# A two-block transformer kernel in float32r: SBUF buffers of matmul operands moved to multiples of 512 bytes

## Chip, cores and metric

The program runs on one core of a Trainium2 chip, in one launch. The metric is device time in microseconds, the median of several executions. In the texts TensorE is PE in the profile's rows, its weight loads PEld, VectorE DVE, ScalarE ACT, GpSimd POOL, and the queue of SyncE SP.

## The reference

One sequence of 512 tokens with 1024 features goes through two blocks of dense products and attention, in float32. Cut to what matters:

```python
def first_block(x, mem, ...):          # two layers
    for i in range(2):
        # layer 0: short convolution with gates, layer 1: window attention with sinks
        y_mem = _mem_attention(q_mem, mk, mv)
        x = x + jnp.concatenate([y_tok, y_mem], -1) @ w_out
        h = rmsnorm(x, norm_ffn[i])
        x = x + (jax.nn.silu(h @ w_gate[i]) * (h @ w_up[i])) @ w_down[i]   # 1024 -> 2816 -> 1024
    return rmsnorm(x, final_norm)

def second_block(x, ...):
    proj = rms_norm(x, norm_pre) @ w_in     # then compressed/causal attention and retention
    merged = sigmoid(m_a) * (y_n @ w_nsa_o) + sigmoid(m_b) * (y_r @ w_ret_o)
    return x + rms_norm(merged @ w_out, norm_post)
```

## The kernel before

Activations lie feature-major: a tile of 128 partitions (features) by 512 columns (tokens), eight such tiles for 1024 features. Every dense product is done to nearly float32's precision with three passes in float32r. Both operands are split into a high part that float32r holds exactly and a low part (the rest), and `mm3` (lines 108 to 113) adds high*high (line 111), high weight*low activation (line 112) and low weight*high activation (line 113) in PSUM. Each of the three is one matmul: its stationary operand, a block of 128x128 weights, is loaded into the array first (a weight load, a row on PEld), and its moving operand, 512 columns of activations, streams through it. So a weight load goes with every matmul, even in line 112, which loads the block that line 111 had loaded.

`proj` (lines 115 to 122) makes a product of 128 output features by 512 tokens: one call of `weights` for a [128, 1024] slab of weights, then three matmuls for each of its eight chunks k, 24 in all (21 or 24 where the hidden layer of a feed-forward part is taken in groups of 8, 7 and 7 chunks). `proj_tok` (lines 124 to 136) is the other way round: it makes 128 tokens by 256 (or 280) features, so that the activations are stationary and 256 columns of weights stream.

`weights` (lines 94 to 106) sets how far ahead the work runs: a DMA on SP brings the slab into one of two buffers `wr`, ScalarE copies it rounded to float32r into one of three buffers `wh` (line 65), VectorE writes the rest into one of three buffers `wl` (line 75). The buffers of a tag go round in turn, so three products in a row use all three pairs of `wh` and `wl`. The order of the work is that of the program as the Tile framework puts it down, with semaphores between engines.

Where the buffers lie: pools are laid out one behind the other in each partition: constants (`cst`, starting at byte 16512), the weight buffers (`wp`), the activation slots (`sl`, mostly of 512 floats, that is 2048 bytes each), and small columns (`sm`). A weight buffer has WMAX = 1120 floats = 4480 bytes, which is 8.75 times 512. The addresses in the built program, with what is left over by 512:

| buffer | address in a partition | modulo 512 |
|---|---|---|
| wh, first, second, third | 34464, 38944, 43424 | 160, 32, 416 |
| wl, first, second, third | 47904, 52384, 56864 | 288, 160, 32 |
| every 2048-byte slot of `sl` (activations, h, q, k, x) | 61344 and on, each a whole number of 2048 | 416 |
| the four `v` slots (values) | 202656 and on | 416 |
| zero, ones; ident | 17792, 17280; 16512 | 384, 384; 128 |

Chunk k of a slab lies 512 k bytes further, so all chunks of a buffer have the same remainder. Products that the steps of the prediction name, by the buffer pair in the built program: the one that starts at 823.58 us uses the third pair, that at 829.13 the second, that at 834.74 the first, that at 840.28 the third again.

Of the kernel before, what the change touches and what calls it, by code (L numbers as in the profile page):

```python
# [8 lines left out]
F32 = mybir.dt.float32  # L9
# [9 lines left out]
D = 1024  # L19
NC8 = 8  # L20
NMEM = 256
NEG = -1.0e30
WMAX = 1120
KWORDS = 2 * 9 * 64
# [3 lines left out]
class Build:  # L28
    """Feature-major activations [128 features, 512 tokens]; every dense product is three float32r
    passes over an exact high/low split of both operands (hi*hi + hi*lo + lo*hi)."""  # L30

# [13 lines left out]

# [1 line left out]
    def nm(self, s):  # L47
# [14 lines left out]

# [1 line left out]
    def copy(self, out, in_, scale=1.0):  # L64
# [14 lines left out]
    def split_one(self, x, tag, scale=None, n=256, name="s"):  # L79
        """Both parts in one tile."""  # L80
        t = self.slot(tag, F32R, (128, KWORDS) if tag == "v" else (128, 512), name)
        hi, lo = t[:, :n], t[:, n:2 * n]
        self.copy(hi, x, 1.0 if scale is None else scale)
        self.lo_of(lo, x, hi, scale)
        return hi, lo
# [8 lines left out]
    def weights(self, src, nk, nn, parts=1):  # L94
        """One load of [128, nk*nn] weights and its split."""
        nc, n = self.nc, nk * nn
        raw = self.wp.tile([128, WMAX], F32, name=self.nm("wr"), tag="wr", bufs=self.wbufs["wr"])
        hi = self.wp.tile([128, WMAX], F32R, name=self.nm("wh"), tag="wh", bufs=self.wbufs["wh"])
        lo = self.wp.tile([128, WMAX], F32R, name=self.nm("wl"), tag="wl", bufs=self.wbufs["wl"])
        step = n // parts  # L100
        for s in (slice(a, a + step) for a in range(0, n, step)):
            nc.sync.dma_start(raw[:, s], src[:, s] if parts > 1 else src)
        for s in (slice(a, a + step) for a in range(0, n, step)):
            self.copy(hi[:, s], raw[:, s])
            self.lo_of(lo[:, s], raw[:, s], hi[:, s])
        v = lambda t: t[:, :n].rearrange("p (k c) -> p k c", k=nk)
        return v(hi), v(lo)
# [7 lines left out]
    def proj(self, ps, src, rhs, w=None, order=None):  # L115
        """ps[128 columns, tokens] = W^T h over all chunks of rhs (8 at most)."""
        n = ps.shape[1]
        wh, wl = w or self.weights(src, len(rhs), 128)
        order = order or range(len(rhs))
        for k in order:  # L120
            ah, al = rhs[k]
            self.mm3(ps, wh[:, k], wl[:, k], ah[:, :n], al[:, :n], k == order[0], k == order[-1])

    def proj_tok(self, src, rhs, nn, ntb, done, nk=4, tag=("pp",)):
        """done(tb, ps[128 tokens, nn]) for each block of 128 tokens."""
        units = [self.weights(src[:, j], nk, nn) for j in range(len(rhs) // nk)]
# [10 lines left out]

# [1 line left out]
    def square_sum(self, chunks, n=512, first=False, gain2=None, tags=("sa", "s")):  # L139
        """The chunks' squares summed by column; with gain2 (squared gains) also their weighted sum."""  # L140
        nc = self.nc
# [18 lines left out]
    def token_mean(self, acc, n, eps, div):  # L160
        """[128 tokens, n/128] of the column sums of acc over div, plus eps."""
        nt = n // 128
# [7 lines left out]
    def rsqrt(self, v):  # L170
        """Newton's iteration from the exponent's halving."""
        nc, n = self.nc, v.shape[1]
# [10 lines left out]
    def newton(self, z, t, y, v):  # L183
        """z = y (1.5 - v y^2 / 2)."""
        self.stt(t, y, -0.5, y, ALU.mult, ALU.mult)
        self.mul(t, t, v)
        self.stt(z, t, 1.5, y, ALU.add, ALU.mult)

    def spread(self, rs, name):
        """[128 tokens, nt] to a row of tokens on every partition."""  # L190
        nc, nt = self.nc, rs.shape[1]
# [12 lines left out]

# [1 line left out]
    def stack_q(self, x):  # L206
        """The two heads of x [128, n], each as its high part on its own half and its low part on the other."""
        n = x.shape[1]
# [8 lines left out]
    def stack_k(self, x, packed=False, tag="b"):  # L217
        """For each head of x [128, n]: its high part on both halves, and its low part on both."""
        n = x.shape[1]
# [22 lines left out]
    def fill_values(self, v, ps, rs):  # L242
        """ps [128 tokens, 4*64] scaled by rs, split, between columns of zeros."""
        hi, lo = v[:, 0, 1::2], v[:, 1, 1::2]
        src = ps.rearrange("p (h c) -> p h c", c=64)
        self.copy(hi, src, rs)
        self.lo_of(lo, src, hi, rs)

    def transposes(self, parts, n):
        """parts: (column, source [128, 128]); the transposed blocks, split."""  # L250
        ps = self.psum("tp")
# [16 lines left out]
    def last_value(self, ps, rs):  # L268
        """The last block of values as they are, for the products too narrow for float32r."""
        v = self.slot("v3", F32, (128, 576), "v3").rearrange("p (j c) -> p j c", c=64)  # L270
# [10 lines left out]
    def scaled(self, p, r):  # L281
        """p *= r, by row."""
        self.nc.vector.tensor_scalar(p, p, r, None, op0=ALU.mult)

# [1 line left out]
    def load_consts(self):  # L286
        nc, T = self.nc, self.T
        self.ident = self.const("ident", [128, 128])
        self.gains = self.const("gains", [128, 8 * 8])
        self.ones = self.const("ones", [128, 128])  # L290
        nc.vector.memset(self.ones, 1.0)
# [26 lines left out]
    def bias_tables(self, loaded):  # L318
        """[128 queries, 12 heads, 256 keys] of the band's bias, -1e30 outside of the window."""
        nc, T = self.nc, self.T  # L320
# [18 lines left out]
    def mem_rows(self, tag="pb"):  # L339
        """The memory times its norm's gain, split; its scale by token at the first call."""  # L340
        nc, T = self.nc, self.T
# [40 lines left out]
    def mem_attention(self, qs, ks, vs):  # L382
        """qs: the two pairs' stacked queries; returns the split outputs of the pairs."""
        nc = self.nc
# [29 lines left out]
    def queries(self, src, h, R, rope=None):  # L414
        """A pair of heads' queries, over 8 and stacked."""
        ps = self.psum("pp")
# [164 lines left out]

# [1 line left out]
    def rope(self, x, tables, shuffle):  # L583
        """x * cos + partner(x) * sin."""
        nc = self.nc
# [17 lines left out]
    def silu(self, ps, R, tag):  # L603
        """z sigmoid(z) as (1 + tanh(z/2)) z/2."""
        z = self.halfsilu_pre(ps, R)
# [5 lines left out]
    def compress(self, kT, j):  # L611
        """The blocks' first product: [2 groups * 31 blocks, 256 hidden]."""
        nc, T = self.nc, self.T
# [25 lines left out]
    def compress_gelu(self, ps, j):  # L639
        """gelu of it, transposed: [128, 2, 2 groups, 32]."""  # L640
        nc = self.nc
# [55 lines left out]
    def cmp_probs(self, g, qpair):  # L697
        """The gated probabilities of group g over the compressed keys, transposed: [4 heads * 32, 512]."""
        nc = self.nc
# [218 lines left out]
    def gate_tanh(self, i, h, R, tag):  # L918
        """tanh of half a merge gate's preactivation: block i // 2 of m_a or m_b."""
        ps = self.psum("pp")  # L920
# [6 lines left out]
    def gate_ahead(self, h, R):  # L927
        """The next merge gate, to DRAM: it keeps TensorE busy beside the softmax."""
        i = len(self.mt)
# [11 lines left out]
    def outer_x(self, c):  # L941
        """Block c of x * gf * rs1, by token, to DRAM."""
        nc = self.nc
# [10 lines left out]
    def finish(self, merged):  # L954
        """out = x * gf * rs1 + rmsnorm(merged @ w_out) by token."""
        nc, T = self.nc, self.T
# [19 lines left out]
        for tb in range(4):  # L976
            v, sd, y0, t, ri = (self.small(1, name=n) for n in ("fv", "fd", "fy", "ft", "fr"))
            nc.vector.tensor_reduce(v, ss[tb], op=ALU.add, axis=AX.X)
# [27 lines left out]

# [1 line left out]
def _feat(w):  # L1008
    """[K, C] to [C/128, 128, K]: per block of columns, each partition's rows of all chunks."""
    k, c = w.shape  # L1010
# [3 lines left out]
def _tok(w, nk=4):  # L1014
    """[K, C] to [128, K/(128 nk), nk*C]."""
    k, c = w.shape
# [3 lines left out]
def _chunks(x):  # L1020
    """[tokens, D] to [128, D/128, tokens]."""
    t, d = x.shape
    return np.ascontiguousarray(x.T.reshape(d // 128, 128, t).transpose(1, 0, 2))
# [36 lines left out]
def _pack(i):  # L1060
    """The arrays that the program reads, laid out."""
    w = {n: np.asarray(a) for n, a in i.items()}
# [62 lines left out]
```

## Time and profile before

| | |
|---|---|
| median of three executions | 1693.08 us (1692.97 to 1693.48) |
| span of the profiled execution | 1692.4 us, 21,221 instructions; of its own time nothing but the span is recorded |
| TensorE busy | 1661.1 us (98%), 8184 matmuls |
| granted TensorE clock, mean | 0.994 |
| weight loads busy | 1378.0 us (81%) |
| VectorE, ScalarE, GpSimd busy | 1055.8, 639.2, 250.5 us |

Matmuls are pipelined. A row's duration runs from its start to a modelled end that lies in the next matmul, so for TensorE's pace one reads the distance from one start to the next; a longer duration shows there too. The weight load of the next matmul runs beside the matmul before it.

### The profile page before, as it was taken

How to read it: one execution, taken by the hardware profiler on the slowest of the kernel's cores; microseconds unless marked ns; L12 is line 12 of the kernel's file. 1: busy time of each engine (PE TensorE's matmuls, PEld its weight loads, DVE VectorE, ACT ScalarE, POOL GpSimd, SP SyncE). 2: the span in 40 equal slices, each digit the busy share in tenths (PEclk: the TensorE clock that was granted, in tenths of full speed). 3: DMA queues.
4: the chain of work that ended last, by engine and by line, in shares of the span. 5: the costliest groups of instructions: out<-in, count | busy, mean ns of one | idle time of the engine just before them, and what ended most of it. 6: DMA issues, size and time to landing. Idle time of an engine off the chain costs nothing.

```text
span 1692.4 us, 21221 instructions
## 1 busy us (share of the span) xinstructions
PE 1661.1 (98%) x8184; PEld 1378.0 (81%) x8184; DVE 1055.8 (62%) x1828; ACT 639.2 (38%) x1134; POOL 250.5 (15%) x220
## 2 busy tenths in 40 slices
PE   8999999999999999999999999999999999999997
PEld 6887878888888788887888888887788888888887
DVE  7765754444454979875434434589788977764444
ACT  5532332222232467633222222334466533333233
POOL 1111411002011600041000101251001000010010
PEclk9999999999999999999999999999999999999999
DMA  5322222322352422122322322332411122143342
GB/s 186 118 83 98 89 89 99 100 88 92 108 168 86 154 90 78 67 100 87 100 89 98 105 95 94 97 135 87 167 41 57 45 81 82 69 149 112 124 157 88
DMA packets 51557, 171.39 MB, mean 101 GB/s; under 512 B 6680, under 2 KB 6880, under 8 KB 51328
## 3 DMA queue, kind: packets, MB, share of 16 engines
q1 hardware_dynamic: 45504, 151.11, 26.4%
q0 software_dynamic: 5376, 18.82, 3.4%
q8 instruction: 64, 1.05, 0.3%
q14 instruction: 37, 0.30, 0.1%
q10 hardware_dynamic: 576, 0.11, 0.0%
HBM read 160.56 MB, written 11.81 MB: 102 GB/s over the span
## 4 chain that ended last, share of the span: by engine, by line
PE 83%; DVE 9%; issue 3%; ACT 2%; DMA 1%; POOL 1%; SPq 0%; DVEq 0%; ACTq 0%; POOLq 0%
PE pp L112 11%; PE pp L113 11%; PE pp L111 11%; PE lg L112 8%; PE lg L113 8%; PE lg L111 7%; PE tp L112 3%; PE tp L113 3%; PE tp L111 3%; PE po L111 2%; PE tp L253 2%; PE po L112 2%; PE po L113 2%; DVE wl L75 2%; PE pp L133 1%
## 5 line engine op out<-in xcount | busy, mean ns | idle before, releaser
L65 ACT ACTIVATE wh<-wr 128x1024 fp32r<-128x1024 f32 (+2 forms) x280 | 288.2, 1029 | 717.9 <-PE pp L112 226.5
L75 DVE TENSOR_TENSOR wl<-wr,wh 128x1024 fp32r<-128x1024 f32 (+2 forms) x280 | 384.6, 1374 | 52.6 <-ACT wh L65 49.4
L111 PE MATMUL pp<-gh,wh 128*128 128x512 f32 x880 | 349.0, 397 | 7.8 <-ACT wh L65 7.2
L113 PE MATMUL pp<-gh,wl 128*128 128x512 f32 x880 | 353.2, 401 | 0.6 <-DVE wl L75 0.6
L112 PE MATMUL pp<-gl,wh 128*128 128x512 f32 x880 | 351.8, 400 | 0.4 <-DVE gl L71 0.4
L111 PEld LDWEIGHTS pp<-gh,wh 128*128 128x128 f32 x880 | 168.9, 192 | 45.7 <-ACT wh L65 8.1
L112 PEld LDWEIGHTS pp<-gl,wh 128*128 128x128 f32 x880 | 166.5, 189 | 37.0 <-DVE gl L71 1.1
L113 PEld LDWEIGHTS pp<-gh,wl 128*128 128x128 f32 x880 | 166.6, 189 | 35.1 <-DVE wl L75 1.6
L113 PE MATMUL lg<-gh,wl 128*128 128x512 f32 x408 | 162.0, 397 | 0.0
L112 PE MATMUL lg<-gl,wh 128*128 128x512 f32 x408 | 161.9, 397 | 0.0
L111 PE MATMUL lg<-gh,wh 128*128 128x512 f32 x408 | 160.6, 394 | 0.0
L68 POOL TENSOR_TENSOR u<-u,z 128x512 f32<-128x512 f32 x44 | 64.6, 1469 | 563.6 <-DVE u L68 375.9
L68 DVE TENSOR_TENSOR u<-lg,Rf 128x512 f32<-128x512 f32 x44 | 30.4, 691 | 144.2 <-PE lg L113 144.1
L111 PEld LDWEIGHTS lg<-gh,wh 128*128 128x128 f32 x408 | 77.7, 190 | 18.5 <-issue 0.5
L112 PEld LDWEIGHTS lg<-gl,wh 128*128 128x128 f32 x408 | 76.6, 188 | 18.9 <-issue 0.7
L113 PEld LDWEIGHTS lg<-gh,wl 128*128 128x128 f32 x408 | 76.6, 188 | 17.1 <-issue 0.2
L112 PE MATMUL tp<-actl,wh 128*128 128x512 f32 x216 | 85.9, 398 | 0.5
L113 PE MATMUL tp<-acth,wl 128*128 128x512 f32 x216 | 85.8, 397 | 0.0
L111 PE MATMUL tp<-acth,wh 128*128 128x512 f32 x216 | 84.4, 391 | 0.0
L68 DVE TENSOR_TENSOR z<-pp,Rf 128x512 f32<-128x512 f32 x44 | 30.4, 691 | 74.6 <-PE pp L113 70.8
L503 DVE TENSOR_TENSOR x<-x,tp 128x512 f32<-128x512 f32 x36 | 24.6, 684 | 68.3 <-PE tp L113 68.3
L71 DVE SCALAR_TENSOR_TENSOR gl<-x,gains,gh 128x512 fp32r<-128x512 f32 x40 | 52.9, 1337 | 0.5 <-ACT gh L65 0.5
(422 smaller groups left out, 3096.6 us busy)
## 6 DMA issues: line engine op xcount, KB each, us to landing
wr<-in_w_gate_dram SPq DMA_DIRECT2D x44, 512.0 KB, 3.2
wr<-in_w_up_dram SPq DMA_DIRECT2D x44, 512.0 KB, 3.2
wr<-in_w_in_dram SPq DMA_DIRECT2D x44, 512.0 KB, 3.3
wr<-in_w_down_dram SPq DMA_DIRECT2D x32, 448.0 KB, 3.3
wr<-in_a_w_in_dram SPq DMA_DIRECT2D x18, 512.0 KB, 3.2
wr<-in_w_down_dram SPq DMA_DIRECT2D x16, 512.0 KB, 3.5
wr<-in_a_w_out_dram SPq DMA_DIRECT2D x8, 512.0 KB, 3.2
wr<-in_b_w_q_dram SPq DMA_DIRECT2D x8, 512.0 KB, 3.2
```

The costliest lines, as they stand in the source:

```text
L65: self.nc.scalar.activation(out, in_, AF.Copy, scale=scale)
L68: (eng or self.nc.vector).tensor_tensor(out, a, b, op=ALU.mult)
L71: (eng or self.nc.vector).scalar_tensor_tensor(out, a, s, b, op0=op0, op1=op1)
L75: self.nc.vector.tensor_tensor(out, x, hi.bitcast(F32), op=ALU.subtract)
L111: mm(ps, ah, bh, start=start, stop=False)
L112: mm(ps, ah, bl, start=False, stop=False)
L113: mm(ps, al, bh, start=False, stop=stop)
L133: mm(ps, a, wh, start=k == 0, stop=False)
L253: self.nc.tensor.transpose(ps[:, c:c + 128], src, self.ident)
L503: nc.vector.tensor_tensor(self.x[c], self.x[c], ps, op=ALU.add)
```

## The change

It puts a constant tile `pad` of 88 floats (352 bytes) behind `gains`, which shifts what follows it; gives the `wh` and `wl` buffers 1152 floats (4608 bytes, 9 times 512) in place of 1120, while `wr`, which no matmul reads, keeps 1120; and takes the five small columns per token block at the end of the program (`fv`, `fd`, `fy`, `ft`, `fr`) from buffers that other steps used earlier, which frees the space. Comments and docstrings are emptied as well.

```diff
-WMAX = 1120
+WMAX = 1152
...
-        raw = self.wp.tile([128, WMAX], F32, name=self.nm("wr"), tag="wr", bufs=self.wbufs["wr"])
+        raw = self.wp.tile([128, 1120], F32, name=self.nm("wr"), tag="wr", bufs=self.wbufs["wr"])
         hi = self.wp.tile([128, WMAX], F32R, name=self.nm("wh"), tag="wh", bufs=self.wbufs["wh"])
         lo = self.wp.tile([128, WMAX], F32R, name=self.nm("wl"), tag="wl", bufs=self.wbufs["wl"])
...
         self.gains = self.const("gains", [128, 8 * 8])
+        self.const("pad", [128, 88])
         self.ones = self.const("ones", [128, 128])
...
-            v, sd, y0, t, ri = (self.small(1, name=n) for n in ("fv", "fd", "fy", "ft", "fr"))
+            v, sd, y0, t, ri = (self.small(4, name=n)[:, :1] for n in ("nm", "den", "es", "rec", "m"))
```

In the built program every engine has the same instructions in the same order, with the same semaphores and waits; only addresses and the row width of `wh`, `wl` and the five columns differ. Now `wh` lies at 34816, 39424 and 44032, `wl` at 48640, 53248 and 57856, and the slots from 62464 on: all of them multiples of 512. Not so the constants: ones and zero have a remainder of 224, ident stays at 128; the small copies `k3` have 256.

## Rows read from the trace of the kernel before

**Rows 1.** The page's span and busy time of each engine.

```profile
span 1692.4 us, 21221 instructions
PE 1661.1 (98%) x8184; PEld 1378.0 (81%) x8184; DVE 1055.8 (62%) x1828; ACT 639.2 (38%) x1134; POOL 250.5 (15%) x220
```

**Rows 2.** The page's chain that ended last, share of the span by engine.

```profile
PE 83%; DVE 9%; issue 3%; ACT 2%; DMA 1%; POOL 1%; SPq 0%; DVEq 0%; ACTq 0%; POOLq 0%
```

**Rows 3.** Engines by stretch: time, then each engine's busy time (count), clock, DMA.

```profile
200.00:560.00 360.00, 359.57 (x1595) 292.79 (x1594) 174.09 (x202) 109.44 (x143) 41.97 (x36) 1.00 0.32 104
...
1560.00:1692.40 132.40, 123.19 (x727) 108.38 (x725) 56.15 (x95) 41.67 (x77) 13.42 (x19) 0.98 0.36 122
```

**Rows 4.** TensorE in time order: start us, us, line; first matmuls of four products.

```profile
823.58 0.39 PE L111 MATMUL pp<-gh,wh 128*128 128x512 f32 x1
...
829.13 0.40 PE L111 MATMUL lg<-gh,wh 128*128 128x512 f32 x1
...
834.74 0.39 PE L111 MATMUL pp<-gh,wh 128*128 128x512 f32 x1
...
840.28 0.39 PE L111 MATMUL lg<-gh,wh 128*128 128x512 f32 x1
```

**Rows 5.** Engines by stretch, 12 to 16 and 800 to 850 (clock after the counts).

```profile
12.00:16.00 4.00, 3.81 (x9) 3.04 (x10) 4.00 (x8) 4.00 (x8) 0.00 (x0) 1.00 0.94 334
800.00:850.00 50.00, 50.00 (x217) 40.69 (x216) 25.75 (x23) 14.81 (x18) 6.45 (x5) 1.00 0.28 90
```

**Rows 6.** TensorE in time order among its first matmuls.

```profile
12.78 0.63 PE L113 MATMUL pp<-gh,wl 128*128 128x512 f32 x1
13.20 0.63 PE L111 MATMUL pp<-gh,wh 128*128 128x512 f32 x1
...
14.91 0.63 PE L112 MATMUL pp<-gl,wh 128*128 128x512 f32 x1
15.34 0.63 PE L113 MATMUL pp<-gh,wl 128*128 128x512 f32 x1
```

**Rows 7.** Lines 111 to 113 in 823.57 to 829.12: duration ns min/median/max.

```profile
L111 PE MATMUL pp<-gh,wh x8: 389/389/390, 823.6 to 828.4; 128*128 128x512 f32 x8
L112 PE MATMUL pp<-gl,wh x8: 396/396/397, 823.8 to 828.7; 128*128 128x512 f32 x8
L113 PE MATMUL pp<-gh,wl x8: 397/397/404, 824.0 to 828.9; 128*128 128x512 f32 x8
```

**Rows 8.** Lines 111 to 113 in 834.73 to 840.28.

```profile
L111 PE MATMUL pp<-gh,wh x8: 389/389/390, 834.7 to 839.6; 128*128 128x512 f32 x8
L112 PE MATMUL pp<-gl,wh x8: 396/396/397, 835.0 to 839.8; 128*128 128x512 f32 x8
L113 PE MATMUL pp<-gh,wl x8: 397/397/397, 835.2 to 840.1; 128*128 128x512 f32 x8
```

**Rows 9.** Lines 111 to 113 in 829.12 to 834.73.

```profile
L111 PE MATMUL lg<-gh,wh x8: 393/393/401, 829.1 to 834.0; 128*128 128x512 f32 x8
L112 PE MATMUL lg<-gl,wh x8: 395/395/398, 829.4 to 834.3; 128*128 128x512 f32 x8
L113 PE MATMUL lg<-gh,wl x8: 393/397/398, 829.6 to 834.5; 128*128 128x512 f32 x8
```

**Rows 10.** TensorE in time order, products of 256 columns: first and last of nineteen.

```profile
599.99 0.28 PE L135 MATMUL pp<-wl,gh 128*128 128x256 f32 x1
...
602.11 0.28 PE L135 MATMUL lg<-wl,gh 128*128 128x256 f32 x1
```

**Rows 11.** The page's costliest groups: the weights' split on ScalarE and VectorE.

```profile
L65 ACT ACTIVATE wh<-wr 128x1024 fp32r<-128x1024 f32 (+2 forms) x280 | 288.2, 1029 | 717.9 <-PE pp L112 226.5
L75 DVE TENSOR_TENSOR wl<-wr,wh 128x1024 fp32r<-128x1024 f32 (+2 forms) x280 | 384.6, 1374 | 52.6 <-ACT wh L65 49.4
```

**Rows 12.** Line 541 (the tile of zeros times itself): duration ns min/median/max.

```profile
L541 PE MATMUL po<-zero x6: 388/392/455, 647.2 to 709.5; 128*128 128x512 f32 x6
```

**Rows 13.** Line 111 alone by product: time, busy (count), loads, clock, DMA share, GB/s.

```profile
823.57:829.12 5.55, 3.11 (x8) 1.54 (x8) 1.00 0.18 38
829.12:834.73 5.61, 3.15 (x8) 1.50 (x8) 1.00 0.45 149
834.73:840.28 5.55, 3.11 (x8) 1.53 (x8) 1.00 0.18 43
840.28:845.84 5.55, 3.11 (x8) 1.54 (x8) 1.00 0.45 149
```

## The prediction

> **What bounds the kernel now.** I read the page first: TensorE is busy for 1661.1 us of a span of 1692.4 [rows 1], and the chain that ended last lies on TensorE for 83%, on VectorE for 9% [rows 2]. The table by stretches says where it is free of everything else: in 200 to 560 us, the first feed-forward part, it is busy for 359.57 us of 360.0; in the last 132 us, where it waits for other engines, for 123.2 [rows 3]. So time is won or lost only by the pace at which matmul follows matmul, and the change can touch nothing else: no instruction, order or wait differs, only addresses.
>
> The pace is in the rows in time order. Three products of 24 matmuls each start at 823.58, 829.13 and 834.74, and the next at 840.28 [rows 4]: 5.55, 5.61 and 5.54 us, 16.70 us for 72 matmuls, or 231.9 ns each, at a granted clock of 1.00 in that part [rows 5]. 512 columns at 2.4 GHz take 213.3 ns. So each matmul pays some 18.6 ns beyond its columns. At the start of the program that is not so: from 12.78 to 15.34 there are six steps of 427 ns [rows 6], just 512 columns at 1.2 GHz, the lower of the two levels (the clock column, with 1.00 in that stretch [rows 5], does not show it). Whatever costs the 18.6 ns is hidden at half the pace.
>
> Now the reader is to see that the extra depends on addresses. The three products are alike but for the buffer pair. In the first, with the third pair, line 111 lasts 389 ns while lines 112 and 113 last 396 and 397 [rows 7]; with the first pair it is the same [rows 8]; with the second pair line 111 lasts 393, up to 401 [rows 9], and the whole product is 0.06 us longer. The activations lie at a remainder of 416 by 512 always, that is 160 by 256. By 256 the remainders of the pairs are: first wh 160 and wl 32, second wh 32 and wl 160, third wh 160 and wl 32. A matmul's length covers the loading of the next block, so the pair to look at is its own block and the next one. Line 111 has wh, then wh again: 160 and 160 in the first and third pairs (fast), 32 and 32 in the second (slow). Line 112 has wh, then wl, line 113 wl, then wh: always one at 160 and one at 32, always slow. So of the nine kinds of step (three lines, three pairs) two are fast: those in which both blocks lie where the activations lie, by 256.
>
> Two sizes follow. With f for a fast step and s for a slow one, the second product is 24 s = 5.61, so s = 233.8 ns; the first is 8 f + 16 s = 5.55, so f = 226 ns. The difference, 7 to 8 ns, agrees with the durations, 389 against 396 or 397 [rows 7]; I take 7, with 6 and 8 as its ends since the rows are rounded to 10 ns.
>
> **The change part by part.** The wider `wh` and `wl` buffers and the `pad` act together: all weight buffers and all slots get the same remainder, 0. Then every matmul has both of its blocks where its activations lie, and by the pattern above every step is a fast one. The program has 5,762 float32r matmuls of 512 columns. Of 72 steps of three products 16 + 24 + 16 = 56 are slow, 78%, which is 4,480 matmuls; at 7 ns each, 31 us on TensorE. Not all of it reaches the end: where TensorE waits for softmax or norms, work done earlier only waits longer. I pass on the chain's share of TensorE, 83%: **26 us**. Ends: 6 ns and 83% give 22, 8 ns and all of it 36.
>
> The 1,676 float32r matmuls of 256 columns: from 599.99 to 602.11 lie 18 steps [rows 10], 118 ns each, against 106.7 for 256 columns. They mix both sorts of addresses already and I see no sorting by them in the rows; price zero, ends zero and 11 ns each, 18.6 us, times 83%: 15 us less.
>
> `wr` moves from remainders 416 and 288 to 256 and 128, so DMAs and the splits in `weights` see other addresses. ScalarE sits idle for 717.9 us before its copies (1029 ns each), and VectorE's subtractions of 1374 ns each run up to three slabs ahead of TensorE [rows 11]; a few ns on 280 of each, 1 or 2 us, would lie under TensorE. If that cover were gone in the feed-forward parts it would be those 2 us. Zero. The five columns in old buffers: they carry no added wait, and a 4-byte column at another address is at most some ns on 20 short instructions of the tail. Zero. ones, zero, ident and `k3` stay off the grid; they serve few matmuls. Zero.
>
> Sum: 1692.4 - 26 = 1666.4 on the profiled execution, which stands 0.7 us under the median of the runs (1693.08): **1667 us** forecast. With the ends of this case alone 1657 to 1672.
>
> **What could lie below.** The fast step, 226 ns, still has 13 ns beyond its columns, and today no activation starts at a multiple of 64 bytes. If the extra is made of steps of some 7 ns and one of them comes from that, all 5,762 lose 7 more: 40 us, times 83%, 33: 1634. The floor is the pace without any extra: 18.6 ns on 5,762, 107 us, times 83%, 89, and 15 from the 256 columns: 1589. The row nearest to the question speaks for staying at 226: line 541 streams the tile of zeros (remainder 384 by 512, a multiple of 128) past itself, and its six matmuls have a median of 392 and a least of 388 ns [rows 12], no shorter than the fast 389. But it streams one block of 128 columns four times, with split weights of either sort behind it, so it is no clean test. The Trainium skill (TensorE: Matmul & The Clock Gate, section Back-to-back issue gap) gives columns over 2.4 plus 2.5 ns between warm matmuls, measured 215.7 for 512 columns. By that figure, as an estimate, 16.2 ns on 5,762 times 83% would go, and the time would be 1615; no row here is that short.
>
> **Rivals.**
>
> Below the fast step: aligned streams and loads shed at least one more step of 7 ns. For it: full pace at the lower clock [rows 6], so the extra is a matter of delivery, which the start of an operand can affect. Against it: [rows 12]. Time 1634, at the extreme 1589; I put 1610 to 1640 on most of it. Chance 0.27.
>
> No change: addresses are not what sets the pace. Then what I read as buffer pairs is something else that alternates with them, the DMA beside TensorE for one: in the product with the second pair the DMA engines were busy for 0.45 of the time, in its neighbours for 0.18 [rows 13]. For it: 0.06 us of 5.55 is a small signal. Against it: the product that starts at 840.28 has a share of 0.45 as well, but the third pair, and there the eight steps of line 111 are back at 3.11 us against 3.15 [rows 13]. Time 1693, within 3. Chance 0.14. The Trainium skill backs this rival (SBUF — State Buffer, section Who interferes with whom): TensorE's two read ports, for the stream and for the loads, are independent, and it never waits on anyone. By that rule the sum would be zero; the rows disagree with it, since line 111 lengthens with the buffer from which blocks are loaded [rows 7, 9].
>
> Slower: remainder 0 is a bad place. That 160 is fast and 32 slow may be a property of the place itself and not of its agreement with the activations: the second pair's line 111 has both blocks at the same place too, and is slow [rows 9]. Loads and streams now all begin at the same phase, and if what delivers them takes turns by address, each pair meets at its first words. It decides if a step with both blocks at 0 takes 234 ns or more. Then the 22% that are fast, 1,280 matmuls, lose 7 ns: 9 us, times 83%, 7: **1700**. If all went to the longest duration of the regular steps, 401 against 396 [rows 9], 5 ns on 5,762 come on top, 24 us with the share: 1724. For it: only one fast place is known. Against it: 160 and 416 are both fast [rows 7, 8], so agreement by 256 explains the rows with one cause. Chance 0.14.
>
> **How the numbers follow.** All steps fast 0.43, below that 0.27, no change 0.14, slower 0.14, the small rest left over. The time is that of the first case, 1667. The range goes down to where 11 of the 13 ns that the fast step has left go too (11 on 5,762, 83%: 53 us under the forecast, 1614) and leaves out what lies lower, about 0.07; at the top it takes in the slow case's first price and leaves out its second, about 0.06: 1614 to 1702, with 1657 to 1672 for the likeliest case alone. A measurement of this kernel can tell about 0.2% from no change, 3.4 us: faster 0.71, same 0.14, slower 0.15.
>
> **What would show it.** Lines 111, 112 and 113 with one and the same duration near 389 ns, for all three buffer pairs; products of 24 matmuls at 5.43 us each, evenly; a stretch of 50 us of feed-forward with 221 matmuls in place of 217 [rows 5]; TensorE's busy time down by some 30 us; the split's means unchanged. The second case shows in durations of 382 and products of 5.28 us or less. I am wrong if the durations still differ between lines with all buffers alike, or if all are at 396 and more.

## The result and the profile after

The changed kernel takes 1670.18 us in the median of four executions (1668.66 to 1670.72), the kernel before 1693.03 us beside it. The ratio is 0.9865, with a 95% interval of 0.9851 to 0.9879: 1.35% faster. The forecast was 1667.

The page of the changed kernel, its span, the engines' busy time and the chain that ended last:

```profile
span 1668.7 us, 21221 instructions
...
PE 1634.9 (98%) x8184; PEld 1374.2 (82%) x8184; DVE 1059.2 (63%) x1828; ACT 639.0 (38%) x1134; POOL 247.1 (15%) x220
...
PE 82%; DVE 10%; issue 2%; ACT 2%; DMA 1%; POOL 1%; DVEq 0%; SPq 0%; ACTq 0%; POOLq 0%
```

Against [rows 1] TensorE is busy for 26.2 us less, and the span is 23.7 us shorter; the kernel has the same bound as before [rows 2]. The same four products as in [rows 4], the first matmul of each, in time order (start us, us, line):

```profile
810.17 0.39 PE L111 MATMUL pp<-gh,wh 128*128 128x512 f32 x1
...
815.61 0.39 PE L111 MATMUL lg<-gh,wh 128*128 128x512 f32 x1
...
821.05 0.39 PE L111 MATMUL pp<-gh,wh 128*128 128x512 f32 x1
...
826.49 0.39 PE L111 MATMUL lg<-gh,wh 128*128 128x512 f32 x1
```

Each product of 24 matmuls takes 5.44 us, whichever buffer pair it uses: 226.7 ns a step, against 231.9 before. Lines 111 to 113 in the first of these products, third pair of buffers (duration ns min/median/max), and in the second, second pair:

```profile
L111 PE MATMUL pp<-gh,wh x8: 389/389/389, 810.2 to 814.9; 128*128 128x512 f32 x8
L112 PE MATMUL pp<-gl,wh x8: 389/389/389, 810.4 to 815.2; 128*128 128x512 f32 x8
L113 PE MATMUL pp<-gh,wl x8: 389/389/389, 810.6 to 815.4; 128*128 128x512 f32 x8
...
L111 PE MATMUL lg<-gh,wh x8: 389/389/389, 815.6 to 820.4; 128*128 128x512 f32 x8
L112 PE MATMUL lg<-gl,wh x8: 389/389/389, 815.8 to 820.6; 128*128 128x512 f32 x8
L113 PE MATMUL lg<-gh,wl x8: 389/389/389, 816.1 to 820.8; 128*128 128x512 f32 x8
```

Where before 389 stood beside 393, 396 and 397 [rows 7, 9], every step now has the one duration that only line 111 with the first and third pairs had. It is the same over the whole program: 140 products of 24 steps run through without a wait. Before, the 92 of them on the first and third pairs took 5.54 to 5.56 us and the 48 on the second pair 5.59 to 5.61; now 134 of the 140 take 5.44. In 800 to 850 us, in the table by stretches (time, busy time and count of each engine, clock, DMA), 222 matmuls stand in place of 217 [rows 5], at the same granted clock of 1.00:

```profile
800.00:850.00 50.00, 50.00 (x222) 41.44 (x221) 24.87 (x24) 14.03 (x17) 5.17 (x4) 1.00 0.31 95
```

The split's groups keep their means, but for 1% on VectorE [rows 11]:

```profile
L65 ACT ACTIVATE wh<-wr 128x1024 fp32r<-128x1024 f32 (+2 forms) x280 | 288.5, 1030 | 695.1 <-PE pp L112 228.0
L75 DVE TENSOR_TENSOR wl<-wr,wh 128x1024 fp32r<-128x1024 f32 (+2 forms) x280 | 388.7, 1389 | 55.5 <-ACT wh L65 52.3
```

One thing got worse. The 18 steps of 256 columns that took 2.12 us [rows 10] take 2.16 now, 120 ns each:

```profile
588.77 0.28 PE L135 MATMUL pp<-wl,gh 128*128 128x256 f32 x1
...
590.93 0.28 PE L135 MATMUL lg<-wl,gh 128*128 128x256 f32 x1
```

### The profile page after: what moved, and what is told of

It is laid out like the page before. It is cut to its first block, busy times and chain, and to the rows that moved or that the text cites. A ratio compares the mean times of both kernels' runs of the same rounds, so it can differ in the third digit from the quotient of the medians.

```text
span 1668.7 us, 21221 instructions
## 1 busy us (share of the span) xinstructions
PE 1634.9 (98%) x8184; PEld 1374.2 (82%) x8184; DVE 1059.2 (63%) x1828; ACT 639.0 (38%) x1134; POOL 247.1 (15%) x220
## 4 chain that ended last, share of the span: by engine, by line
PE 82%; DVE 10%; issue 2%; ACT 2%; DMA 1%; POOL 1%; DVEq 0%; SPq 0%; ACTq 0%; POOLq 0%
PE pp L112 11%; PE pp L113 11%; PE pp L111 11%; PE lg L111 8%; PE lg L112 8%; PE lg L113 7%; PE tp L112 3%; PE tp L253 2%; PE tp L113 2%; PE tp L111 2%; DVE wl L75 2%; PE po L111 2%; PE po L112 2%; PE po L113 2%; PE pp L133 2%
## 5 line engine op out<-in xcount | busy, mean ns | idle before, releaser
L75 DVE TENSOR_TENSOR wl<-wr,wh 128x1024 fp32r<-128x1024 f32 (+2 forms) x280 | 388.7, 1389 | 55.5 <-ACT wh L65 52.3
L113 PE MATMUL pp<-gh,wl 128*128 128x512 f32 x880 | 347.2, 395 | 0.6 <-DVE wl L75 0.6
L112 PE MATMUL pp<-gl,wh 128*128 128x512 f32 x880 | 346.7, 394 | 0.5 <-DVE gl L71 0.5
L504 DVE TENSOR_TENSOR x<-x,tp 128x512 f32<-128x512 f32 x36 | 24.6, 683 | 65.5 <-PE tp L113 65.5
```

The source lines that it names most:

```text
L75: self.nc.vector.tensor_tensor(out, x, hi.bitcast(F32), op=ALU.subtract)
L112: mm(ps, ah, bl, start=False, stop=False)
L113: mm(ps, al, bh, start=False, stop=stop)
L504: nc.vector.tensor_tensor(self.x[c], self.x[c], ps, op=ALU.add)
```

## The experiments

All of them are edits of the changed kernel. "Distance" below is the address of the stationary block less that of the stream, by 256 bytes: 0, 256 and 512 bytes apart are one distance, and so are -64 and 192.

**The two halves of the change.** First the wider buffers without the pad, then the pad without the wider buffers.

```diff
# e1_wide_only
-        self.const("pad", [128, 88])
# e2_pad_only
-WMAX = 1152
+WMAX = 1120
```

> The change without its pad: wh and wl are 1152 floats wide, so weight buffers and slots all have the remainder 160 by 512, not a multiple of 512 nor of 64. Theory A (a step is fast when its own block and the next one lie where the stream lies, by 256): every step fast, about 227 ns, time as with the whole change, 1670 us. Theory M (the multiple of 512 is what counts): the slow steps stay, 1693 us.

> The change without the wider buffers: 1120 floats and the pad. wh lies at 0, 384, 256 by 512, wl at 128, 0, 384, slots at 256. Relations by 256 are those of before (wh agrees, differs by 128, agrees; wl the opposite). Theory A: 1693 us, line 111 fast in two of three products. Theory P (the place of the weight blocks alone counts, 0 and 160 by 256 being good ones): not sure to repeat before's pattern, since 128 by 256 has not been seen; theory M: between, the slots being off the grid.

e1_wide_only: 1670.52 us (1669.00 to 1671.99), ratio to before 0.9867, 0.9850 to 0.9883. Weights and slots all lie at 160 by 512, and the products follow each other as in the whole change, 5.44 us apart:

```profile
811.13 0.39 PE L111 MATMUL pp<-gh,wh 128*128 128x512 f32 x1
...
816.57 0.39 PE L111 MATMUL lg<-gh,wh 128*128 128x512 f32 x1
```

e2_pad_only: 1691.97 us in one execution, before's time. Line 111 in two products, then line 112 in the first (duration ns min/median/max):

```profile
L111 PE MATMUL pp<-gh,wh x8: 389/389/389, 823.5 to 828.3; 128*128 128x512 f32 x8
L111 PE MATMUL lg<-gh,wh x8: 393/393/401, 829.0 to 834.0; 128*128 128x512 f32 x8
...
L112 PE MATMUL pp<-gl,wh x8: 396/396/396, 823.7 to 828.6; 128*128 128x512 f32 x8
```

The medians are those of before to the nanosecond, with every address moved. So the wider buffers carry the gain, the pad carries none, and a multiple of 512 is not what counts: theory M falls.

**Is it the place or the agreement?** e3_slots_128 leaves all weight blocks on multiples of 512 and moves the activation slots alone (with the small columns behind them, which no dense product reads); e4_all_32 puts everything at 32 by 256, where the slow blocks of before had lain.

```diff
# e3_slots_128, in weights, behind lo
+        if "gap2" not in self.wbufs:
+            self.wbufs["gap2"] = self.wp.tile([128, 32], F32, name="gap2", tag="gap2", bufs=1)
# e4_all_32
-        self.const("pad", [128, 88])
+        self.const("pad", [128, 32])
```

> The whole change, and 128 bytes of padding behind the weight buffers, so that all weight blocks stay at multiples of 512 and all activation slots lie 128 bytes off. Theory A: no step agrees with its stream, all are slow, 233 to 235 ns; 5,762 steps at 7 ns, 83% of it: 33 us above the change, 1703 us. Theory P (the weight blocks' place alone): all fast, 1670 us.

> The wider buffers and a pad of 32 floats: weight buffers and slots all at 288 by 512, that is 32 by 256, where before's slow blocks lay. Theory A: all agree, all fast, 1670 us. Theory P: 32 by 256 is a bad place for a weight block, all steps 233 ns or more, 1700 us.

e3_slots_128 took 1695.56 us, e4_all_32 1669.59, one execution each, where the change took 1670.18. The page of e3_slots_128 and the starts of its four products (two lines are added ahead of `mm3`, so line 113 is what line 111 was):

```profile
span 1693.8 us, 21221 instructions
...
PE 1663.2 (98%) x8184; PEld 1375.1 (81%) x8184; DVE 1056.3 (62%) x1828; ACT 640.6 (38%) x1134; POOL 251.1 (15%) x220
```

```profile
825.35 0.39 PE L113 MATMUL pp<-gh,wh 128*128 128x512 f32 x1
...
842.08 0.39 PE L113 MATMUL lg<-gh,wh 128*128 128x512 f32 x1
```

72 steps in 16.73 us, 232.4 ns each, with no weight block moved; TensorE is busy for 28.3 us more than in the change. And in e4_all_32, in the place that had been slow, the same products are 5.44 us apart:

```profile
810.02 0.39 PE L111 MATMUL pp<-gh,wh 128*128 128x512 f32 x1
...
815.46 0.39 PE L111 MATMUL lg<-gh,wh 128*128 128x512 f32 x1
```

Theory P falls from both sides; theory A holds in these four runs. Its price for e3_slots_128, 1703, was 7 us too high: without agreement the steps lie anywhere between 228 and 241 ns, mean 232.4, and not all at 234.

**How near is near?** Other distances: 64 bytes for all, then buffers that step by 64 and by 32 bytes.

```diff
# e5_slots_64: as e3_slots_128, with [128, 16]
# e6_pitch_64: gap2 of [128, 96], and
-WMAX = 1152
+WMAX = 1136
# e7_pitch_32: gap2 of [128, 48], and
-WMAX = 1152
+WMAX = 1144
```

> The whole change with 64 bytes of padding behind the weight buffers: weight blocks at multiples of 512, slots 64 bytes off. Theory A1 (fast only at a distance of 0 by 256): all steps slow, 1695 us as with 128 bytes. Theory A2 (the extra comes from the 128 bytes in which a block starts, so 64 bytes off is still the same place): 1670 us.

> Weight buffers 4544 bytes apart, so that with the slots at 0 by 512 the three wh lie at 0, -64, -128 and the three wl at -192, -256, -320. Read by step, not by time: line 111 has own and next block alike. A1: 227 ns with the first pair, 230 or more with the second and third. A2: fast with the first, and with the second where -64 counts as near. If any distance takes out more than agreement does, some step stands under 226 ns. Time between 1685 and 1700 us.

> The same with buffers 4576 bytes apart: wh at 0, -32, -64, wl at -96, -128, -160 against the slots. A1: line 111 fast with the first pair alone. A2: fast with -32 as well. A step under 226 ns would show that less than the 13 ns extra is to be had by some other distance. Time between 1680 and 1700 us.

e5_slots_64: 1676.68 us in one execution, neither of the two times. Its 72 steps take 16.48 us, 228.9 ns each:

```profile
814.33 0.39 PE L113 MATMUL pp<-gh,wh 128*128 128x512 f32 x1
...
830.81 0.39 PE L113 MATMUL lg<-gh,wh 128*128 128x512 f32 x1
```

Inside a product the three steps of a chunk take 226, 229 and 232 ns, chunk after chunk. Which line has which changes from product to product, though the blocks and streams of all lines lie at the same distance: of the 140 whole products 88 begin with the 226, 43 with the 232 and 9 with the 229. So here a single step's length does not tell the price of its own addresses; the product's does, 5.49 or 5.50 us in all 140.

e6_pitch_64 took 1687.80 us, e7_pitch_32 1688.90, one execution each. The high-by-high line of e6_pitch_64 in three products, with wh at -128, -64 and 0 from the stream:

```profile
L113 PE MATMUL pp<-gh,wh x8: 387/396/404, 820.3 to 825.1; 128*128 128x512 f32 x8
L113 PE MATMUL lg<-gh,wh x8: 392/393/394, 825.8 to 830.6; 128*128 128x512 f32 x8
L113 PE MATMUL pp<-gh,wh x8: 389/389/390, 831.3 to 836.2; 128*128 128x512 f32 x8
```

In this run the line lengthens with the distance. In e7_pitch_32 it does not; its rows of the same line with wh at -64 and at 0 (third and first pair):

```profile
L113 PE MATMUL pp<-gh,wh x8: 388/389/398, 821.1 to 825.9; 128*128 128x512 f32 x8
L113 PE MATMUL pp<-gh,wh x8: 392/393/393, 832.2 to 837.1; 128*128 128x512 f32 x8
```

The pair that agrees is the longer one, against A1 and A2 alike: from start to start, 231.0 ns a step with a distance of 0 and 229.4 with -64. So where all blocks lie equally far from their streams, the price grows with the distance (226.7, 228.9 and 232.4 ns at 0, 64 and 128 bytes), but neither A1 nor A2 is the whole law, and a step's own and next block do not settle it alone. Counted over the whole program, for steps of line 111 (113 in e6 and e7) with both blocks at a distance of 0, the mean is 227.2 ns in before, 227.3 in the change, but 228.7 in e6_pitch_64 and 231.2 in e7_pitch_32, where the blocks around them lie otherwise. What in those sets it stays open. No distance has a mean under the 227 of full agreement, though single steps in e5 and e6 come down to 225.

**The 256-column products.** In e5_slots_64 they took 18 steps in 2.04 us:

```profile
592.51 0.28 PE L137 MATMUL pp<-wl,gh 128*128 128x256 f32 x1
...
594.55 0.28 PE L137 MATMUL lg<-wl,gh 128*128 128x256 f32 x1
```

So a version with agreement in the products of 512 columns and a distance of 64 in `proj_tok`, measured beside the change on the same chip:

```diff
# f1_tok_192 (f2_tok_64: off=16)
-    def weights(self, src, nk, nn, parts=1):
+    def weights(self, src, nk, nn, parts=1, off=0):
...
+        hi, lo = hi[:, off:off + n], lo[:, off:off + n]
...
-        units = [self.weights(src[:, j], nk, nn) for j in range(len(rhs) // nk)]
+        units = [self.weights(src[:, j], nk, nn, off=48 if nn == 256 else 0) for j in range(len(rhs) // nk)]
```

> The change as it is, on the chip of the next runs, to compare with them: 1670 us, steps of 512 columns at 227 ns, of 256 columns at 119 ns.

> The change, and in proj_tok's products of 256 columns the weights begin 192 bytes into their buffer, so that the stationary activations lie 64 bytes off the stream, by 256, as in e5_slots_64, where these steps took 116 ns against 119 in the change. Agreement holds as before in the 512 column products. If the distance between load and stream sets both: 1,676 steps at 3 ns, 5 us less than the change, 1665 us. If 116 there came from something else: 1670 us.

> The same with 64 bytes in place of 192: the distance is then 192 by 256, the other way round. If the distance counts in both directions alike: 1665 us; if the direction matters: 1670 us or somewhat more.

The change again: 1669.82 us (1669.62 to 1671.47), ratio to before 0.9867, 0.9851 to 0.9884. f1_tok_192: 1667.37 us (1666.85 to 1668.48), 0.9851, 0.9836 to 0.9866. f2_tok_64: 1668.50 us (1668.03 to 1669.46), 0.9857, 0.9843 to 0.9872. f1's four executions all lie below the change's four; it is the fastest float32r version that ran, by 2.5 us, half of what was expected. The 18 steps in f1_tok_192:

```profile
586.81 0.28 PE L136 MATMUL pp<-wl,gh 128*128 128x256 f32 x1
...
588.93 0.28 PE L136 MATMUL lg<-wl,gh 128*128 128x256 f32 x1
```

2.12 us, as in before [rows 10], against 2.16 in the change; the 2.04 of e5_slots_64 was not reached, though the distance by 256 is the same. What else differs is the absolute place of the stream (192 against 0). A good part of the missing gain was never there to be had: the edit moves the distance in the 960 matmuls of `proj_tok` with 256 columns, not in all 1,676 that the expectation counts. The mean of those went from 119.9 ns in the change to 116.1 in f1 and 116.9 in f2, against 115.1 in e5; 3.8 ns on 960 is 3.6 us. The other products of 256 columns stay where they were, at 118.7 to 118.9 ns. Both directions help, so f2's rival, that the direction matters, is not supported beyond its 1 us.

**What is left beyond the columns.** The fast step keeps 13 ns over 213.3. Here every float32r operand becomes a bfloat16 one (high and low parts of 8 bits each, a less exact computation), with weights and slots agreeing, then with the slots 128 bytes off.

```diff
# g2_bf16 (and all bitcasts of high parts to F32 dropped); g3_bf16_128 adds gap2 of [128, 32]
-F32R = mybir.dt.float32r
+F32R = mybir.dt.bfloat16
-WMAX = 1152
+WMAX = 1280
```

> Every float32r operand is a bfloat16 one (high and low parts of 8 bits each, so products are less exact; three passes as before), buffers agreeing by 256. It asks what the 13 ns beyond 213 are that agreement leaves. If they come from reading 4-byte operands (the conflict of loads and streams that agreement only reduces): steps of 512 columns at about 216 ns, 5,762 times 11 ns, some 55 us less than the change, 1615 us. If they are a fixed cost of going from one weight block to the next: 227 ns and 1670 us, but for faster or slower splits on VectorE and ScalarE.

> The bfloat16 kernel with 128 bytes of padding behind the weight buffers, so that blocks and streams disagree by 128 as in e3_slots_128. If the whole extra belongs to 4-byte operands: steps of 512 columns stay at 216 ns, time as without the padding, 1603 us. If places matter for 2-byte operands too: steps of some 220 ns and more, 1620 us or above.

g2_bf16: 1602.61 us in one execution. Its first product and the next, and the weight loads of line 111 in the first (duration ns min/median/max):

```profile
778.01 0.38 PE L111 MATMUL pp<-gh,wh 128*128 128x512 bf16 x1
...
783.19 0.38 PE L111 MATMUL lg<-gh,wh 128*128 128x512 bf16 x1
```

```profile
L111 PEld LDWEIGHTS <-wh x8: 97/97/98, 778.4 to 783.0; 128*128 128x128 bf16 x8
```

5.18 us for 24 steps, 215.8 ns each, as the first case had it. The time is 12 us under its 1615: the 256-column steps, which it left out, fell as well, from 119.4 to 109.2 ns, some 16 us. g3_bf16_128: 1598.19 us, also in one execution, and again 5.18 us:

```profile
775.26 0.38 PE L113 MATMUL pp<-gh,wh 128*128 128x512 bf16 x1
...
780.44 0.38 PE L113 MATMUL lg<-gh,wh 128*128 128x512 bf16 x1
```

With two-byte operands the 128 bytes that cost 25 us in e3_slots_128 cost nothing. So most of the 13 ns, and all of the dependence on address at these two distances, belongs to four-byte operands. Both the stream and the loads changed (a load mostly lasts 97 or 98 ns in place of 187 to 192), so which of the two it is stays open.

## Why the prediction was right

**The bound** and **the pattern of nine kinds of step** were read rightly: two kinds fast, those in which own and next block lie where the stream lies by 256, and e2_pad_only repeats them at other addresses. As a law for single steps the pattern is too simple, as e5_slots_64 and e7_pitch_32 show; what the forecast needed, that all steps are fast once all blocks agree with all streams, holds. That forecast came out to the nanosecond: 389 in all lines and pairs, 5.44 us a product where 5.43 was said, 222 matmuls in 50 us where 221 was said.

**The sum** was 26 us; the span fell by 23.7. That they come so close is in part luck: two terms were too favourable, and a third, the share that passes on, was too low and made up for most of it. (The upper end of the likeliest case is a slip: 22 us less gives 1671, not 1672.) The counts below go from the start of a matmul to the start of the next.

- *Slow steps, 4,480 at 7 ns, 31 us.* Of all matmuls of 512 columns, before has 4,401 with a step between 229 and 246 ns, mean 233.5, and 1,169 fast ones (220 to 228) at 226.6: 6.8 ns on 4,401 is 29.9 us. In the change 548 steps are still in that band, mean 233.1, which keeps 3.5 us. Each of them lies within ten matmuls of one of another length or of a wait; in 200 to 550 us, where products of 512 columns run through, they are 29 of 1,467 steps. The prediction took every step for one inside a product. That leaves 26.4 us.
- *256 columns, zero.* Over all regular steps (100 to 130 ns) their mean rose from 118.2 to 119.4 ns: 1.8 us against the change. The row of 2.12 us that had been read as indifferent mixed distances. In `proj_tok` before, the steps at a distance of 0 took 117.7 ns and those at 128 took 118.2; now all are at 0 and take 119.9, and all at 128 in e3_slots_128 take 119.4. Why a mixture is quicker than either stays open.
- *83% passes on.* 26.4 less 1.8 is 24.6, and the span fell by 23.7: nearly everything passes. TensorE's waits and steps of other lengths took 1.5 us more, and the first matmul started 0.5 us earlier. The chain's share of TensorE says how long the chain lies on it, not how much of a gain on it reaches the end.

The split, `wr` and the five columns were put at zero. VectorE's mean rose by 15 ns on 280, some 4 us beside a busy TensorE; whether any of the 1.5 us comes from it is not shown.

**The rivals.** *No change* falls with the result, and with e3_slots_128, where 128 bytes between stream and blocks and nothing else that a dense product reads cost 25 us. The Trainium skill (SBUF — State Buffer, section Who interferes with whom) says that TensorE's stream and loads have ports of their own and that it never waits on anyone; for two-byte operands this case agrees (g3_bf16_128, 215.8 ns at a distance of 128), for float32r the measurement speaks against it (232.4 ns at that distance, 226.7 at 0). *Slower, remainder 0 a bad place* falls with the change, which lies at 0, and with e4_all_32, which lies at 32: both take 5.44 us a product. *Below the fast step* was wrong as put: an aligned start takes out nothing beyond agreement, since e1_wide_only at 160 by 512 is as fast as the change at 0. The Trainium skill's 215.7 ns (TensorE: Matmul & The Clock Gate, section Wait — 56ns, not 53.3ns?) is what the bfloat16 runs show, with 215.8; float32r with agreement stands 11 ns above it, and no distance that ran had a product under 5.44 us.

## What to carry to other kernels

With float32r matmuls back to back, look at the starts from one product to the next by buffer: if the pace follows which rotating buffer is in use, make the distance between the stationary blocks and the streams a multiple of 256 bytes, by the buffers' pitch. Where the buffers lie in absolute terms made no difference here, so the pad was not needed. Products of 256 columns can want another distance than those of 512, so measure each kind. Where one engine is the bound nearly throughout, as TensorE is here, expect most of a gain on it to reach the end: 23.7 of 24.6 us in this case.

## What the hardware showed that was not expected

- The address dependence is graded: with all blocks equally far from their streams, the 512-column steps of three products take 226.7 ns at a distance of 0, 228.9 with 64 bytes, 232.4 with 128. With mixed distances a step depends on more than its own and the next block (e7_pitch_32).
- Products of 256 columns in `proj_tok` are slower with agreement (119.9 ns a step) than in e5_slots_64 with 64 bytes between (115.1).
- The address dependence is gone with two-byte operands: 215.8 ns at distances of 0 and of 128 alike, with weight loads of 97 or 98 ns in place of 187 to 192.
